# Attention's list with the last value group and the first output weights in it, measured durations, and both ScalarE tables loaded ahead of their stages

## The chip, the cores and the metric

One core of a Trainium2 chip runs the whole layer; seven stay unused. The metric is the device time of one execution in microseconds (us). TensorE is PE in the tables (its weight loads PEld), VectorE DVE, ScalarE ACT, GpSimd POOL, and SyncE SP, which issues nearly all DMAs. Every recorded operation goes through one helper, so nearly all rows carry line 183 (DMAs 177); they are told apart by their tiles.

## The reference

A decoder layer for 1024 tokens of width 1024. What matters here is the mixer:

```
h = x * (1 + scale1) + shift1
q, k, v, u, iq, ik, iw = split(h @ w_in)            # 8 heads of 64, 512 pooling channels, an indexer
score = sum over 8 index heads of iw * relu(rope(iq) @ rope(ik).T / 8), causal
keep the 256 highest scores of each token
p = softmax(rope(q) @ rope(k).T / 8 over the kept tokens);  attn = p @ v
x = layer_norm(alpha * x + gate1 * (concat(attn, pooled) @ w_o))
x = layer_norm(alpha * x + gate2 * ((silu(h2 @ w_gate) * (h2 @ w_up)) @ w_down))
```

## The kernel before, in words

Tokens are eight tiles of 128 (tile 7 is the last). Products are float32 split into a high and a low part, three matmuls for one; a split is an ACT copy (high) and a subtraction on DVE or POOL (low). The order of the instructions on an engine is that of the program where the engine is in the set `pinned`; where it is not, the framework may move an instruction ahead.

First come the modulation and the indexer's scores. For each tile from 2 to 7 the 256th highest score is then searched in generators (`bisect`, `mask_steps`, `drop_eights`), which yield the engine and cost of their next step. Tiles 7 and 6 are searched on DVE, 5 and 4 and then 3 on ACT by Sign activations, tile 2 on DVE by dropping eights (17 passes of a maximum and a replacement). The end of each is the mask: an equality, a count, a scan and 16-bit products, which write the bias for the softmax over the scores.

Beside the searches PE works through 24 `groups`: eight of pooling, eight of k, eight of v (loop of `PAIRS`); a function `fill` puts search steps into the holes that a running estimate of time (`Times`, `Queue.cost`) sees. A group is 24 matmuls of 512 columns. In the last group, number 23, `hold` stops the Sign steps and all chains but that of tile 7.

Attention is then a list. There are 32 units, a pair of heads (even and odd) by a tile of queries, grouped by g = 3, 2, 1, 0 (tiles 7 and 6, 5 and 4, and so on). A unit is a chain of tasks: s (scores, PE), x (bias and maximum, DVE, one for each head), e (exponent with its sum, ACT), r (reciprocal, DVE), n (norm, POOL), p (transposes, PE), c (copy out of PSUM, ACT or DVE), and for each two units o (values, PE) with hi (ACT) and lo (DVE). q tiles 5 to 0 come back from DRAM and are turned (load on SP, turn on PE, own and other on ACT, low on DVE). What is left of the three search chains are Chain objects in the same list. The list goes by one loop: each task's earliest time follows from the clocks of its engine and from its inputs' modelled ends; of those within SPAN us of the earliest, the one of lowest rank (its place in the units plus PRIO of its kind; for chains CHAIN_PRIO's first value plus a step for each of theirs) is written out. V_BIAS is added to a copy's time on DVE when the two engines are compared. Scores take two buffers of PSUM (ring B, two slots for over 512 columns), the others four (ring A). TensorE, DVE, ACT and POOL are pinned in the list.

The scaled probabilities lie in smr and the transposed ones in ptb, both in area H over hT, which group 23 still reads. Behind the list come the output weights: wo_load (an SP load, and a multiplication by gate1 on POOL) and wo_split, WO[0] and WO[1] in area V, the rest over k and v. Raw weights and q tiles share three buffers (RAW). After the list, weights are unpinned. The output projection starts with three tiles' products, k by k; then normalisation and the FFN, whose first Silu stands far behind.

Of the kernel before, what the change touches and what calls it, by code (L numbers as in the profile page):

```python
# [20 lines left out]
P = 128  # L21
# [22 lines left out]
V_BIAS = -0.075  # L44
SPAN = 0.106
PRIO = {'load': -387, 'turn': -49, 'own': -168, 'low': -13, 'other': -88, 's': 3, 'x': -36, 'e': 1, 'r': 152, 'n': -121, 'p': 12, 'c': 332, 'o': -134, 'hi': -115, 'lo': 145}
CHAIN_PRIO = {2: (500, 22.3), 3: (347, 6.4), 4: (-732, 10.2)}
# [148 lines left out]
def decoder_layer_kernel(  # L196
# [376 lines left out]
    def mask_steps(i, T1, ng, eq, lt):  # L573
        n, sc, w = P * (i + 1), score(i), (i + 1) / 8
        yield "V", 1.7 * w + 0.1
# [4 lines left out]
        yield "V", 1.6 * w  # L580
# [3 lines left out]
        yield "V", 1.8 * w  # L584
# [5 lines left out]
    def drop_eights(i, cols):  # L590
# [6 lines left out]
        for r in range((n - TOPK) // 8):  # L597
            yield "V", 1.0
            V.max(m8, neg)
            V.match_replace(neg, m8, neg, -3.4e38)  # L600
# [421 lines left out]
    last = len(groups)  # L1022
    pinned.clear()
# [12 lines left out]
    for s_ in (last, last + 1):  # L1036
        for f in late.pop(s_, []):
            f()
    assert not late, late
    def cat_slot(g):  # L1040
        return WS[g]
# [80 lines left out]
    def wo_load(k):  # L1122
        wo_raw[k] = raw_slot()
        SP.dma_start(wo_raw[k], wo_in[k])
        G.tensor_tensor(wo_raw[k], wo_raw[k], GR, ALU.mult)

# [57 lines left out]
    q_done, q_turns = {7: (), 6: ()}, []  # L1184
    masked = {0: 0.0, 1: 0.0}

    def q_rows(t, rank):
# [27 lines left out]
        t_ = task("turn", "T", 0.55, rank, turn, (l_,), "A", late=0.2)  # L1215
# [4 lines left out]
        t_.masks = {1: (3,), 0: (4, 5)}.get(t, ())  # L1220
        q_done[t] = (c1, lw)
        q_turns.append(t_)

    def unit(k):
# [31 lines left out]
        for e in (0, 1):  # L1256
            for j0 in range(0, i + 1, 4):
# [17 lines left out]
                c = task("c", "AV", (0.09 + 0.11 * m, 0.09 + 0.13 * m), 10 * k + 3, c_, [p] + list(o_tasks[-2:-1]), late=0.1)  # L1275
# [11 lines left out]
    for k in range(0, nu, 2):  # L1287
# [14 lines left out]
        o_t = task("o", "T", 0.1 + 0.865 * (g + 1), 10 * k + 14, o_, cs, "A", late=0.3)  # L1302
# [4 lines left out]
    class Chain:  # L1307
# [5 lines left out]
        def step(self):  # L1313
# [48 lines left out]
    while todo or chains:  # L1362
# [768 lines left out]
```

## Time and profile before

| what | value |
|---|---|
| median of 3 runs | 1252.07 us (1249.63 to 1252.88) |
| the profiled execution | 1250.99 us, of it 1249.2 us span of instructions |
| busy: PE, DVE, ACT, POOL | 1180.4, 1002.0, 656.0, 709.3 us |
| group 23 | about 328 to 334 us of the span |
| attention's list | about 334 to 472 us |
| output projection | from 468 us |
| ACT table loads | 4 of 1.28 us |

A profile's times are those of one execution. Busy time of PE is not its peak: matmuls overlap, their duration in a row is their latency. The granted clock is the share of PE's full clock: 1.0 is 2.4 GHz, 0.5 is 1.2 GHz, and a value between them is a mean of stretches at either.

### The profile page before, as it was taken

How to read it: one execution, taken by the hardware profiler on the slowest of the kernel's cores; microseconds unless marked ns; L12 is line 12 of the kernel's file. 1: busy time of each engine (PE TensorE's matmuls, PEld its weight loads, DVE VectorE, ACT ScalarE, POOL GpSimd, SP SyncE). 2: the span in 40 equal slices, each digit the busy share in tenths (PEclk: the TensorE clock that was granted, in tenths of full speed). 3: DMA queues.
4: the chain of work that ended last, by engine and by line, in shares of the span. 5: the costliest groups of instructions: out<-in, count | busy, mean ns of one | idle time of the engine just before them, and what ended most of it. 6: DMA issues, size and time to landing. Idle time of an engine off the chain costs nothing.

```text
span 1249.2 us, 16310 instructions
## 1 busy us (share of the span) xinstructions
PE 1180.4 (94%) x5622; PEld 919.8 (74%) x5622; DVE 1002.0 (80%) x1772; ACT 656.0 (53%) x1330; POOL 709.3 (57%) x505
## 2 busy tenths in 40 slices
PE   8999989999888899997899999999999999999996
PEld 6756556687665568876778787877878787878775
DVE  6799997988989975686977878787777768687698
ACT  4667878787789683455343434333333333442521
POOL 0093484676034362286784838475665748486848
PEclk9999999999989899997999999999999999999998
DMA  9610167421101035001312111112102020213212
GB/s 349 251 49 11 47 242 280 154 70 60 43 1 35 34 134 174 39 9 34 102 34 68 34 68 34 68 34 67 68 34 72 32 99 23 81 34 101 68 51 118
DMA packets 32459, 103.40 MB, mean 83 GB/s; under 512 B 3572, under 2 KB 3572, under 8 KB 28792
## 3 DMA queue, kind: packets, MB, share of 16 engines
q1 hardware_dynamic: 32376, 102.36, 23.1%
q8 instruction: 44, 0.72, 0.2%
q14 instruction: 39, 0.32, 0.1%
HBM read 92.90 MB, written 9.45 MB: 82 GB/s over the span
## 4 chain that ended last, share of the span: by engine, by line
PE 38%; DVE 7%; POOL 5%; issue 2%; ACT 1%; DVEq 0%; POOLq 0%; ACTq 0%
PE gu L183 23%; PE dn L183 15%; DVE act_W L183 2%; DVE utmp_X L183 2%; POOL wraw_R L183 1%; POOL wblk_T L183 1%; POOL wraw_W L183 1%; POOL wblk_V L183 1%; DVE gtmp_V L183 1%; DVE wblk_T L183 1%; DVE hr_H L183 0%; POOL hr_H L183 0%; DVE stat_C L183 0%; DVE wblk_V L183 0%; DVE res_X L183 0%
## 5 line engine op out<-in xcount | busy, mean ns | idle before, releaser
L183 PE MATMUL gu<-hr_H,wblk_T 128*128 128x512 f32 (+1 forms) x924 | 216.9, 387 | 2.6 <-ACT gtmp_V L183 2.3
L183 PE MATMUL gu<-hr_H,wblk_V 128*128 128x512 f32 (+1 forms) x924 | 215.1, 384 | 2.4 <-ACT gtmp_V L183 1.7
L183 PEld LDWEIGHTS gu<-hr_H,wblk_T 128*128 128x128 f32 x924 | 171.7, 190 | 38.7 <-ACT gtmp_V L183 2.9
L183 PEld LDWEIGHTS gu<-hr_H,wblk_V 128*128 128x128 f32 x924 | 170.0, 188 | 38.6 <-ACT gtmp_V L183 2.2
L183 DVE TENSOR_TENSOR res_X<-res_X,dn 128x512 f32<-128x512 f32 (+1 forms) x253 | 158.5, 675 | 15.4 <-PE dn L183 15.3
L183 POOL TENSOR_TENSOR wraw_R<-wraw_R 128x512 f32<-128x512 f32 x64 | 93.9, 1475 | 45.8 <-DVE wblk_T L183 23.1
L183 POOL TENSOR_TENSOR wraw_W<-wraw_W 128x512 f32<-128x512 f32 x60 | 85.8, 1437 | 55.8 <-DVE wblk_V L183 27.4
L183 PE MATMUL pj<-ws_W,hT_H 128*128 128x512 f32 x456 | 115.7, 400 | 1.0 <-DVE ws_W L183 1.0
L183 POOL TENSOR_SCALAR sm_H<-sm_H,stat_X 128x1024 f32<-128x1024 f32 (+7 forms) x64 | 49.1, 783 | 96.9 <-DVE stat_X L183 83.0
L183 PEld LDWEIGHTS pj<-ws_W,hT_H 128*128 128x128 f32 x456 | 83.0, 188 | 24.9 <-issue 6.5
L183 PE MATMUL dn<-wblk_T,act_W 128*128 128x512 f32 x324 | 79.4, 393 | 1.9 <-POOL wblk_T L183 1.2
L183 PE MATMUL dn<-wblk_V,act_W 128*128 128x512 f32 x324 | 78.8, 392 | 1.1 <-POOL wblk_V L183 1.1
L183 DVE TENSOR_SCALAR_CACHE_REDUCE junk_X<-keysD_T,colsD_X 128x1024 int16<-128x1024 int16 (+1 forms) x64 | 79.4, 1268 | 0.2
L183 ACT ACTIVATE wblk_V<-wraw_R 128x512 fp32r<-128x512 f32 x56 | 35.2, 629 | 80.7 <-POOL wraw_R L183 69.1
L183 PEld LDWEIGHTS dn<-wblk_T,act_W 128*128 128x128 f32 x324 | 60.1, 188 | 17.4 <-POOL wblk_T L183 3.9
L183 ACT ACTIVATE wblk_V<-wraw_W 128x512 fp32r<-128x512 f32 x53 | 33.1, 628 | 75.9 <-POOL wraw_W L183 62.4
L183 PEld LDWEIGHTS dn<-wblk_V,act_W 128*128 128x128 f32 x324 | 60.2, 188 | 16.2 <-POOL wblk_V L183 3.9
L183 ACT ACTIVATE wblk_T<-wraw_W 128x512 fp32r<-128x512 f32 x56 | 35.0, 628 | 65.9 <-POOL wraw_W L183 53.8
L183 ACT ACTIVATE wblk_T<-wraw_R 128x512 fp32r<-128x512 f32 x52 | 32.5, 627 | 61.3 <-POOL wraw_R L183 51.3
L183 PE MATMUL pT<-const_C,sm_H 128*128 128x128 f32 x288 | 45.2, 299 | 15.7 <-POOL sm_H L183 8.2
L183 DVE SCALAR_TENSOR_TENSOR score_X<-relu_K,const_C,score_X 128x384 f32<-128x384 f32 (+5 forms) x42 | 54.1, 1289 | 5.0 <-ACT relu_K L183 1.3
L183 ACT ACTIVATE utmp_X<-gu 128x512 f32<-128x512 f32 x33 | 19.7, 598 | 73.0 <-PE gu L183 73.0
(301 smaller groups left out, 2717.4 us busy)
## 6 DMA issues: line engine op xcount, KB each, us to landing
mset_K<-in_wmr_dram SPq DMA_DIRECT2D x16, 1024.0 KB, 5.3
wm_K<-in_wma_dram SPq DMA_DIRECT2D x16, 512.0 KB, 10.2
wraw_R<-in_wg_dram SPq DMA_DIRECT2D x6, 1024.0 KB, 4.7
wraw_R<-in_wd_dram SPq DMA_DIRECT2D x12, 512.0 KB, 3.6
wraw_W<-in_wup_dram SPq DMA_DIRECT2D x12, 512.0 KB, 3.5
wraw_R<-in_wup_dram SPq DMA_DIRECT2D x10, 512.0 KB, 3.6
wraw_W<-in_wg_dram SPq DMA_DIRECT2D x5, 1024.0 KB, 4.8
wraw_W<-in_wd_dram SPq DMA_DIRECT2D x10, 512.0 KB, 3.5
```

The costliest lines, as they stand in the source:

```text
L183: ins_ = f(*a, **k)
```

## The change

Group 23 leaves the loop and becomes the task vg of the list (with the copies va of group 22 and vb of group 23). Unit 0 has buffers of its own (sm_first). The x of later units, the first copies c, and turns of q tiles above 2 wait for vg. Loads and gates of output weights 0 to 2 and the splits of 0 and 1 become tasks; SP stays pinned in the list; a load is not written out before the one in front of it. Costs, ranks, V_BIAS and SPAN change. Ahead of a transposition p with a foreseen hole of more than 0.5 us on PE, KEEP times the rest of the hole is filled with transposes of the identity. One-column activations load ACT's tables: Exp at group 22, Silu at the end of the list.

```diff
-V_BIAS = -0.075
-SPAN = 0.106
-PRIO = {'load': -387, 'turn': -49, 'own': -168, 'low': -13, 'other': -88, 's': 3, 'x': -36, 'e': 1, 'r': 152, 'n': -121, 'p': 12, 'c': 332, 'o': -134, 'hi': -115, 'lo': 145}
-CHAIN_PRIO = {2: (500, 22.3), 3: (347, 6.4), 4: (-732, 10.2)}
+V_BIAS = 0.15
+KEEP = 0.55
+SPAN = 0.15
+PRIO = {'load': 650, 'turn': 53, 'own': -1350, 'low': -687, 'other': 600, 's': -261, 'x': -1371, 'e': 71, 'r': -915, 'n': 1966, 'p': -227, 'c': 659, 'o': -951, 'hi': -1034, 'lo': 641, 'gate': -895, 'group': 863, 'take': 1269, 'whi': -1001, 'wlo': -635}
+CHAIN_PRIO = {2: (1157, 15.6), 3: (1224, 52.0), 4: (1044, 55.3)}
...
-        yield "V", 1.7 * w + 0.1
+        yield "V", 1.7 * w + 0.1, False, 1.7 * w + 0.5
...
-        yield "V", 1.6 * w
+        yield "V", 1.6 * w, False, 3.4 * w
...
-        yield "V", 1.8 * w
+        yield "V", 1.8 * w, False, 2.9 * w
...
-            yield "V", 1.0
+            yield "V", 1.24
...
-    for n_, (kind, a, b) in enumerate(groups):
-        if n_ == len(groups) - 1:
-            hold.append(1)
+    for n_, (kind, a, b) in enumerate(groups[:-1]):
...
+        if n_ == 22:
+            at_(n_, lambda: A.activation(colsE[:, 16:17], ident[:, 0:1], AF.Exp))
...
-    last = len(groups)
-    pinned.clear()
+    last = len(groups) - 1
...
+    (take_22,) = late.pop(last)
+    sm_first = [buf("X", 5312, 1024, "sm"), buf("V", 7168, 1024, "sm")]
...
+    vg = task("group", "T", 3.4, 0, group_23, (), "A", late=0.2)
+    va = task("take", "A", 0.55, 0, take_22, (), late=0.1)
+    vb = task("take", "A", 0.55, 0, lambda: v_take(groups[-1][1], got["pp"]), (vg,), late=0.1)
...
-        t_ = task("turn", "T", 0.55, rank, turn, (l_,), "A", late=0.2)
+        t_ = task("turn", "T", 0.55, rank, turn, (l_, vg) if t > 2 else (l_,), "A", late=0.2)
...
-        s_t = task("s", "T", 0.2 + 0.0014 * n, 10 * k - EAGER, s_, q_done[i], "B" if n <= 512 else "BB", late=0.2)
+        s_t = task("s", "T", 0.1 + 0.0014 * n, 10 * k - EAGER, s_, q_done[i], "B" if n <= 512 else "BB", late=0.2)
-        xs = [task("x", "V", 0.08 + 0.00105 * n, 10 * k, lambda e=e: x_(e), [s_t] + before, late=0.12) for e in (0, 1)]
+        xs = [task("x", "V", 0.08 + 0.00105 * n, 10 * k, lambda e=e: x_(e), [s_t] + before + [vg] * (k > 0), late=0.12) for e in (0, 1)]
...
+                    for _ in range(spare):
+                        T.transpose(pt[:, 0:P], ident, ident)
...
-                c = task("c", "AV", (0.09 + 0.11 * m, 0.09 + 0.13 * m), 10 * k + 3, c_, [p] + list(o_tasks[-2:-1]), late=0.1)
+                c = task("c", "AV", (0.09 + 0.11 * m, 0.09 + 0.13 * m), 10 * k + 3, c_, [p] + (list(o_tasks[-2:-1]) or [vg]), late=0.1)
...
+        if k == 0:
+            turns[2].deps = list(turns[2].deps) + ps
...
-        o_t = task("o", "T", 0.1 + 0.865 * (g + 1), 10 * k + 14, o_, cs, "A", late=0.3)
+        o_t = task("o", "T", 0.865 * (g + 1) - 0.1, 10 * k + 14, o_, cs + [va, vb] * (g == 3), "A", late=0.3)
...
-            self.cost = (0.95 if self.q == "A" else 1.08) * self.st[1][1]
+            self.cost = self.st[1][3] if len(self.st[1]) > 3 else (0.9 if self.q == "A" else 1.02) * self.st[1][1]
...
+    for k in range(3):
+        d_ = task("load", "S", 0.1, 200, lambda k=k: wo_dma(k), (q_turns[3 + k],), late=5.0)
+        g_ = task("gate", "G", 2.35, 200 + k, lambda k=k: wo_gate(k), (d_,), late=0.15)
+        if k < 2:
+            h_ = task("whi", "A", 1.05, 205 + k, lambda k=k: wo_hi(k), [g_] + o_tasks[3:4], late=0.1)
+            task("wlo", "V", 1.15, 206 + k, lambda k=k: wo_lo(k), (h_,))
...
+        if t.kind == "p":
+            gap = at - max(clock[q], rings["A"].ready(1))
+            spare = max(0, int(KEEP * (gap - 0.5) / 0.11))
...
+    A.activation(colsE[:, 17:18], ident[:, 0:1], AF.Silu)
     pinned.clear()
-    wo_load(0)
-    wo_split(0)
-    wo_load(1)
-    wo_load(2)
     times.fill = None
-    wo_split(1)
     wo_split(2)
```

## Rows read from the trace of the kernel before

**Rows 1.** Windows of attention's list. Columns: the stretch, its length, then for PE, PEld, DVE, ACT and POOL the busy time and in brackets the instructions, then the granted clock, the DMA share and GB/s.
```profile
334.00:345.00 11.00, 7.39 (x36) 4.69 (x34) 8.30 (x19) 10.72 (x21) 2.22 (x2) 0.81 0.22 73
345.00:360.00 15.00, 11.72 (x59) 8.34 (x58) 13.28 (x27) 12.93 (x26) 4.20 (x4) 0.80 0.00 0
360.00:380.00 20.00, 19.20 (x152) 13.79 (x151) 18.93 (x45) 18.12 (x43) 8.48 (x8) 1.00 0.00 2
380.00:400.00 20.00, 17.83 (x139) 12.06 (x137) 17.61 (x43) 18.02 (x44) 7.78 (x7) 1.00 0.12 39
400.00:420.00 20.00, 17.27 (x111) 11.67 (x111) 18.55 (x45) 14.89 (x37) 10.69 (x8) 0.83 0.11 42
420.00:440.00 20.00, 15.28 (x89) 10.21 (x90) 19.28 (x53) 13.44 (x31) 9.46 (x10) 0.91 0.08 27
440.00:460.00 20.00, 20.00 (x164) 14.04 (x166) 14.71 (x48) 14.89 (x45) 13.04 (x19) 1.00 0.52 185
460.00:472.50 12.50, 12.29 (x92) 8.50 (x89) 7.08 (x38) 9.26 (x38) 4.99 (x12) 1.00 0.24 86
```

**Rows 2.** PE's timeline at the start of the list: start, length, engine, operation, and in brackets the idle time before it with its releaser. The first row holds groups 22 (end) and 23.
```profile
322.69 11.18 PE L183 MATMUL pj<-ws_W,hT_H 128*128 128x512 f32 x48
...
342.60 1.11 PE L183 MATMUL pT<-const_C,sm_H 128*128 128x128 f32 x4 [2.84 <-POOL sm_H L183]
...
348.76 0.63 PE L183 MATMUL pT<-const_C,sm_H 128*128 128x128 f32 x4 [1.15 <-ACT qab_W L183]
...
352.08 0.66 PE L183 MATMUL pT<-const_C,sm_H 128*128 128x128 f32 x4 [0.95 <-DVE pT_H L183]
353.87 4.70 PE L183 MATMUL pT<-const_C,sm_H 128*128 128x128 f32 x26 [1.13 <-DVE pT_H L183]
```

**Rows 3.** ACT's timeline around it: a Sign step (junkB), the last copy of v, the table load and the first exponent.
```profile
323.10 0.72 ACT L183 ACTIVATE junkB_X<-keysA_X,colsA_X 128x512 bf16<-128x512 uint16 x1 [1.54 <-DVE colsA_X L183]
...
333.91 0.60 ACT L183 ACTIVATE vf_V<-pj 128x512 f32<-128x512 f32 x1 [4.42 <-PE pj L183]
...
337.38 1.28 ACT L183 ACT_TABLE_LOAD   x1
338.67 1.15 ACT L183 ACTIVATE sm_H<-sm_H,stat_X 128x1024 f32<-128x1024 f32 x1
```

**Rows 4.** DVE's timeline, the two largest holes of 334 to 345 us.
```profile
341.08 0.17 DVE L183 RECIPROCAL stat_X<-stat_X 128x2 f32<-128x2 f32 x1 [0.85 <-ACT sm_H L183]
...
344.57 2.81 DVE L183 TENSOR_TENSOR qab_W<-qT,qab_W 64x512 fp32r<-64x512 f32 x4 [1.32 <-ACT qab_W L183]
```

**Rows 5.** Groups of instructions over the whole run, the table loads: busy time, mean ns, idle time before and its releasers.
```profile
L183 ACT ACT_TABLE_LOAD x4 | 5.1, 1283 | 2.6 <-DVE gtmp_V L183 1.8 <-PEq L2119 0.7
```

**Rows 6.** The tile pT, its copies on both engines: shortest, median and longest in ns, first and last start.
```profile
L183 ACT ACTIVATE pT_H<-pT x51: 262/493/616, 354.9 to 471.1; 128x512 f32<-128x512 f32 x24, 128x384 f32<-128x384 f32 x10, 128x128 f32<-128x128 f32 x9, 128x256 f32<-128x256 f32 x8
L183 DVE COPY pT_H<-pT x45: 270/670/692, 351.3 to 470.9; 128x512 f32<-128x512 f32 x24, 128x256 f32<-128x256 f32 x8, 128x128 f32<-128x128 f32 x7, 128x384 f32<-128x384 f32 x6
```

**Rows 7.** The tile raw from 280 to 480 us, the gate multiplications of output weights, columns as in rows 6.
```profile
L183 POOL TENSOR_TENSOR raw_R<-raw_R,gr_G x5: 2367/2372/2391, 389.3 to 451.2; 128x1024 f32<-128x1024 f32 x5
```

**Rows 8.** Timelines of POOL, then DVE, then PE about 417 us: a gate, mask steps of tile 3, PE's next work.
```profile
417.14 2.37 POOL L183 TENSOR_TENSOR raw_R<-raw_R,gr_G 128x1024 f32<-128x1024 f32 x1 [2.92 <-PE pT L183]
...
417.35 2.44 DVE L183 TENSOR_TENSOR keysA_X<-keysA_X,score_X 128x512 bf16<-128x512 bf16 x1
419.83 0.43 DVE L183 TENSOR_TENSOR junkB_X<-junkB_X,keysA_X 128x512 bf16<-128x512 bf16 x1
...
422.40 2.21 PE L183 MATMUL pT<-const_C,sm_H 128*128 128x128 f32 x10 [3.34 <-POOL sm_H L183]
```

**Rows 9.** Timelines of POOL, then DVE: the next gate, and the mask steps of tile 2 from its scan on.
```profile
429.14 2.39 POOL L183 TENSOR_TENSOR raw_R<-raw_R,gr_G 128x1024 f32<-128x1024 f32 x1 [5.91 <-issue]
...
426.00 1.01 DVE L183 TENSOR_TENSOR_SCAN score_X<-neg_X,colsE_X 128x384 bf16<-128x384 bf16 x1
427.05 0.26 DVE L183 TENSOR_SCALAR score_X<-score_X 128x384 bf16<-128x384 bf16 x1
...
430.21 1.54 DVE L183 TENSOR_TENSOR neg_X<-neg_X,score_X 128x384 bf16<-128x384 bf16 x1
431.78 0.94 DVE L183 TENSOR_TENSOR neg_X<-neg_X 128x384 bf16<-128x384 bf16 x1
432.76 0.95 DVE L183 TENSOR_SCALAR score_X<-neg_X 128x384 f32<-128x384 bf16 x1
```

**Rows 10.** ACT's timeline in the FFN, the last table load and the first Silu.
```profile
589.86 1.28 ACT L183 ACT_TABLE_LOAD   x1 [1.81 <-DVE gtmp_V L183]
591.15 0.72 ACT L183 ACTIVATE gtmp_V<-gtmp_V 128x256 f32<-128x256 f32 x2
```

**Rows 11.** PE's timeline behind it.
```profile
593.82 1.22 PE L183 MATMUL gu<-hr_H,wblk_V 128*128 128x256 f32 x8 [0.36 <-POOL hr_H L183]
596.42 3.92 PE L183 MATMUL gu<-hr_H,wblk_T 128*128 128x256 f32 x18 [1.38 <-ACT gtmp_V L183]
```

**Rows 12.** Timelines of ACT and PE at the end of the list: the splits of weights 2 to 4, and PE's first matmuls with weights 2 and later (tile hr).
```profile
472.64 2.94 ACT L183 ACTIVATE hr_H<-raw_R 128x1024 fp32r<-128x1024 f32 x3
...
478.96 7.42 PE L183 MATMUL wo<-hr_H,ws_W 128*128 128x512 f32 x32
```

**Rows 13.** PE's timeline after the mask of tile 2.
```profile
435.11 1.16 PE L183 MATMUL s<-kr_K,qab_H 128*128 128x512 f32 x4 [0.90 <-DVE stat_X L183]
```

More of the change, by code (lines that the diff above doesn't have):

```diff
@@ L1035, in decoder_layer_kernel @@
     smr = buf("H", 8192, 6144, "sm")
-    for s_ in (last, last + 1):
-        for f in late.pop(s_, []):
-            f()
+    (take_22,) = late.pop(last)
     assert not late, late
+    sm_first = [buf("X", 5312, 1024, "sm"), buf("V", 7168, 1024, "sm")]
     def cat_slot(g):
@@ L1120, in decoder_layer_kernel, with wo_dma, wo_gate, wo_load @@
     wo_raw = {}
-    def wo_load(k):
+    def wo_dma(k):
         wo_raw[k] = raw_slot()
         SP.dma_start(wo_raw[k], wo_in[k])
+    def wo_gate(k):
         G.tensor_tensor(wo_raw[k], wo_raw[k], GR, ALU.mult)
+    def wo_load(k):
+        wo_dma(k)
+        wo_gate(k)
     def wo_split(k):
@@ L1144, in pool_split @@
             V.tensor_tensor(lo, src, f_(hi), ALU.subtract)
+    loads = []
     class Task:
@@ L1149, in __init__ @@
             self.q, self.cost, self.rank, self.emit, self.deps, self.slots, self.late = q, cost, rank + PRIO[kind], emit, deps, slots, late
-            self.end, self.kind, self.masks = None, kind, ()
+            self.end, self.kind, self.masks, self.behind = None, kind, (), loads[-1:] if kind == "load" else []
+            if kind == "load":
+                loads.append(self)
     class Ring:
@@ L1176, in decoder_layer_kernel @@
         n = P * (u[2] + 1)
-        if n > 512:
+        if u == units[0]:
+            sm_of[u] = sm_first, {6}
+        elif n > 512:
             sm_of[u] = [smr[:, (o + e) % 6 * 1024 :][:, 0:n] for e in (0, 1)], {o % 6, (o + 1) % 6}
@@ L1183, in decoder_layer_kernel, with group_23 @@
     sm_users, live = {}, {}
-    q_done, q_turns = {7: (), 6: ()}, []
+    q_done, q_turns, turns = {7: (), 6: ()}, [], {}
     masked = {0: 0.0, 1: 0.0}
+    got = {}
+    def group_23():
+        got["pp"] = psA("pj")
+        t_f(groups[-1][1])(got["pp"], range(KT))
+    vg = task("group", "T", 3.4, 0, group_23, (), "A", late=0.2)
+    va = task("take", "A", 0.55, 0, take_22, (), late=0.1)
+    vb = task("take", "A", 0.55, 0, lambda: v_take(groups[-1][1], got["pp"]), (vg,), late=0.1)
+    vg.readers = (vb,)
+    rings["A"].free[-1][0] = 1.0
     def q_rows(t, rank):
@@ L1220, in q_rows @@
         t_.masks = {1: (3,), 0: (4, 5)}.get(t, ())
+        turns[t] = t_
         q_done[t] = (c1, lw)
@@ L1259, in unit, with p_ @@
                 hold_ = {}
-                def p_(e=e, j0=j0, m=m, hold_=hold_):
+                def p_(spare=0, e=e, j0=j0, m=m, hold_=hold_):
                     hold_["pt"] = pt = psA("pT")
+                    for _ in range(spare):
+                        T.transpose(pt[:, 0:P], ident, ident)
                     for j in range(m):
@@ L1317, in step, with wo_hi, wo_lo @@
             self.q = self.st[1][0]
-            self.cost = (0.95 if self.q == "A" else 1.08) * self.st[1][1]
+            self.cost = self.st[1][3] if len(self.st[1]) > 3 else (0.9 if self.q == "A" else 1.02) * self.st[1][1]
+    def wo_hi(k):
+        A.activation(WO[k][:, 0:1024], wo_raw[k], AF.Copy)
+    def wo_lo(k):
+        V.tensor_tensor(WO[k][:, 1024:2048], wo_raw[k], f_(WO[k][:, 0:1024]), ALU.subtract)
+    for k in range(3):
[4 more added lines that the diff above has]
+            task("wlo", "V", 1.15, 206 + k, lambda k=k: wo_lo(k), (h_,))
     t0 = T.t
@@ L1335, in earliest @@
             at = max(at, d.end)
+        if any(b.end is None for b in t.behind):
+            return FAR
         for i in t.masks:
@@ L1380, in decoder_layer_kernel @@
             kind[0] = t.kind
+        spare = 0
+        if t.kind == "p":
+            gap = at - max(clock[q], rings["A"].ready(1))
+            spare = max(0, int(KEEP * (gap - 0.5) / 0.11))
         if t.slots:
             t.got = rings[t.slots[0]].take(len(t.slots))
-        t.emit(q) if len(t.q) > 1 else t.emit()
+        if spare:
+            t.emit(spare)
+        else:
+            t.emit(q) if len(t.q) > 1 else t.emit()
         clock[q] = at + cost
```

## The prediction

> **What bounds the kernel now.** I read first the windows of the attention stage, then PE's timeline there, then ACT's and DVE's around each PE hole, last the place of the FFN where the second table is loaded. The windows say that the stage has two limits [rows 1]. From 334 to 440 us DVE is busy 8.30 + 13.28 + 18.93 + 17.61 + 18.55 + 19.28 = 95.95 of 106 us, ACT 88.12, PE 88.69; PE's share moreover holds half-clock work (mean granted clock 0.80 to 0.83 in three of the stretches). From 440 us on PE is full (20.00 of 20.00, 12.29 of 12.50) and DVE has air. So up to 440 us the list is worth what it saves on DVE; after that PE's work (32.5 us) can only begin earlier. PE can follow such a shift: it sits idle 106 - 88.69 = 17.3 us before 440.
>
> The stage's start is the worst part. Group 23 (half of the 11.18 us row of 48 matmuls, 5.6 us) ends at 333.9, only then does unit 0 begin, and its chain scores, x, exponent, norm, transpose must run through before the pipe is full: PE waits 2.84, 1.15, 0.95 and 1.13 us, partly at half clock [rows 2]. On ACT the Sign steps are held back during group 23 (4.42 us idle), and the exponent's table is loaded between the first x and the first exponent, 1.28 us [rows 3]. DVE's idle time from 334 to 360 us is 2.70 + 1.72 = 4.42 us [rows 1]; its pieces end with ACT's results [rows 4].
>
> **The change, part by part.**
>
> *Group 23 in the list.* Unit 0's scores need nothing of the group, and by the list's rule (earliest first, then rank) they go out before it; unit 0 now has buffers outside hT's area, the x of all others wait for the group. So x, exponent and norm of unit 0 run beside 5.6 us of PE work instead of beside a waiting PE. The bound is DVE, whose work does not shrink: what can go is its idle time, 4.42 us. Ends: 0 (the hole only moves) and 5.6 (the whole group hidden). I take 4.4, nearer to the upper end, since PE's holes alone (6.07 us) exceed the group.
>
> *Exponent's table.* Its load goes to group 22, where ACT had a hole of 1.54 us ahead of a Sign step [rows 3]; if that hole is gone it costs a Sign chain 1.28 us, and PE nothing. The gain lies in the 4.4 already. Relu, Sign and Copy alternate with exponents and Silu in the whole kernel at four loads [rows 5], so nothing is reloaded. The lifted hold on the Sign chain, 4.4 us of ACT, is credited with nothing: ACT is not the bound.
>
> *Copies.* The bias of 0.15 us against DVE (before 0.075 for it) sends copies of transposed probabilities to ACT. 45 run on DVE, median 0.67 us, the largest 0.69; on ACT the largest take 0.62 [rows 6]. The busy times differ by 95.95 - 88.12 = 7.8 us [rows 1], one moved large copy closes 0.69 + 0.62 = 1.31, so six level them and take 4.1 us off DVE. Ends 0 and 4.1; I take four median copies, 2.7 us, since some will meet an ACT that is not free.
>
> *Output weights 0 to 2 in the list.* Three loads on SP, three gate multiplications on POOL of 2.37 us [rows 7], two splits on ACT and DVE. All ran within the attention before, put there by the framework, so no work is added. Behind a gate on POOL stand the norms, and behind them PE's transposes; behind a load on SP, which keeps its order in the list now, only the next loads. The danger is what a gate meets. The one at 417.14 ran beside a DVE mask step of two 16-bit inputs: 2.44 us, where the next of the same shape took 0.43; PE then stood still for 3.34 us until the norm came [rows 8]. Beside the gate at 429.14 and the norm behind it the last three steps of tile 2 took 1.54, 0.94 and 0.95 [rows 9]. Against the 0.43 of the larger tile that is 1.11 + 0.51 + 0.52 = 2.1; with the 2.0 at 417 it is 4.1 us of DVE. The Trainium skill (GPSIMD Engine Reference, Key points) says that GpSimd shares its SBUF interfaces with VectorE and contends with its two-input and two-port instructions: the trace agrees with 2.44 against 0.43, and by that rule gates fixed in the list speak against the change wherever they fall on mask steps. Where they fall now the trace cannot show. Ends: 4.1 gained (no meeting) and 4.1 lost (two more); I take 0, since as many gates and mask steps remain.
>
> *Durations, ranks.* A drop step costed at 1.08 us becomes 1.26 (1.24 x 1.02), mask steps up to double. I credit that with nothing of its own: it brings the list nearer to the chip, but DVE, busy 95.95 of 106 us [rows 1], leaves little to order. Ends: the 5.6 us of DVE idle time from 360 to 440 us gained, or as much again lost.
>
> *Spare transposes.* PE transposes the identity ahead of a foreseen hole, to hold the clock. The 0.81 and 0.80 granted from 334 to 360 us [rows 1] mean about 10.2 us at 1.2 instead of 2.4 GHz, 5.1 us of PE work, but PE is not the bound there. Ends: 2.2 us gained (DVE's idle time from 400 to 440 us, the other stretches of a lowered clock) and 1.1 us lost (six spare ones at the 0.18 us of the 26 transposes at 353.87 [rows 2], ahead of holes that don't come). I take 0: PE's 17.3 idle us hide them; without that cover they cost the 1.1.
>
> *Silu's table.* The load leaves the FFN. At 589.86 it stands between DVE's product and the first Silu [rows 10]; PE waits 0.36 and 1.38 us for work that queued behind it [rows 11]. Ends 0 and 1.28; I take 1.2, as the waits exceed it. The new place is the end of the list: 472.6, ahead of the split of weights 2, the first of three on ACT of about 1 us each; PE needs it at 478.96 [rows 12]. With a DVE half of about the same length it is done by 476.4 instead of 474.9. So 1.5 us of 4 us of cover are used; if that cover were gone it would cost 1.5.
>
> The Trainium skill (ScalarE: Activation LUTs, What ACT_TABLE_LOAD costs) puts a drain of about 1.38 us on top of each load. By it the two loads would be worth 5.3 us in place of 2.6, and the time would be an estimated 1.4 us lower, for Silu's alone. The rows at 337 and 589 show 1.28 us and the next ACTIVATE at once [rows 3, 10]; the measurement decides.
>
> **Sum.** 4.4 + 2.7 + 1.2 = 8.3 us. The profiled execution took 1250.99 (span 1249.2 and 1.8 around it), 1.1 below the median of the three runs, 1252.07, inside their spread. 1250.99 - 8.3 = **1242.7 us**.
>
> **Rivals.**
>
> *The masks come late (slower).* Chains rank behind everything in the list now (from 1044 upward, copies from 662 to 972), so DVE takes a chain step only when nothing else is ready. Scores of units 16 and 17 do not wait for masks, their x do: if masks 3 and 2 are not there when units 0 to 15 are through, both score buffers fill with waiting scores and PE stops. For it: PE already waited 0.90 us for such a buffer at 435.11, just after mask 2 [rows 13]. Against it: the list plans those steps, with longer costs than before. It decides once the last steps stand alone on DVE. Price: scan to bias of tile 2 uncovered, 1.01 + 0.26 + 1.54 + 0.94 + 0.95 = 4.7 [rows 9], and of tile 3 by its length 4/3 of that, 6.3, an estimate; moved copies then bring nothing: 1250.99 - 4.4 - 1.2 + 11.0 = 1256.4.
>
> *The gain at the start is given back.* Unit 0 starts early, but the x of unit 1 waits for group 23 as before, so the hole appears behind it; copies moved to ACT make its exponents late. For it: only unit 0 has buffers of its own, and ACT is busy 88.12 of 106 us [rows 1]. Only Silu's 1.2 remains: 1249.8.
>
> *The list as a whole gets better.* No gate on a mask step, six copies moved: 5.6 + 4.1 + 4.1 + 1.28 = 15.1, so 1235.9. For it: PE has 17.3 idle us to give [rows 1]. Against it: all ends at once.
>
> *It does not do what it says.* A table load that stays where it was, or a second one by a later exponent: 1.28 or 2.6 us less gain, 1244.0 or 1245.3, within the forecast's own case.
>
> **Numbers.** Forecast 0.60 (with the last rival in it), whole list better 0.10, given back 0.18, masks late 0.12. A measurement of this kernel can tell about 0.3% from no change, 3.8 us. The first two are faster, 0.70; the third is the same, 0.18; the last slower, 0.12. Range: from 1236 (nearly all gain ends) to 1254, which takes in given back and the lesser half of masks late.
>
> **What would show it.** Right: scores of unit 0 ahead of the matmuls of group 23, the first PE hole after them under 1 us, clock 1.0 through the first 25 us; no table load at the first exponent nor at the first Silu; fewer than 45 copies on DVE; stage end 7 us earlier, and FFN stretches of the same length but for 1.2 us. Wrong: as much DVE idle time up to the masks as before, PE idle around masks 3 and 2 by several us, or gates that lengthen mask steps again.

## The result and the profile after

The kernel after takes 1238.99 us (median of 5 runs, 1238.61 to 1241.15) against 1252.07 before: ratio 0.990, interval 0.9886 to 0.9915, a gain of 12.5 us (10.6 to 14.3). Measured again later, unchanged (run e9), it took 1242.14 (6 runs, 1238.63 to 1244.00) against 1251.37: ratio 0.9922 (0.9904 to 0.994), a gain of 9.8 us (7.5 to 12.0). The forecast was 1242.7, faster; both medians lie in its range. The profiled execution took 1238.72 (span 1236.7), 12.27 below the profiled one before.

Where the 12.3 us of the two profiled executions came from can be read at three places. PE's first matmul with weights 2 (tile hr) starts at 466.15 instead of 478.96 [rows 12]: 12.8 us are gained by the end of the list. The stage of the output projection (wo) gives 1.6 of it back. The FFN gains 1.1 around its first Silu. The windows of the list, in the stretches and columns of [rows 1]:

```profile
334.00:345.00 11.00, 7.37 (x40) 4.70 (x38) 10.80 (x22) 9.69 (x19) 2.23 (x2) 1.00 0.14 49
345.00:360.00 15.00, 14.27 (x94) 10.17 (x95) 12.94 (x30) 14.43 (x27) 7.37 (x8) 0.89 0.06 17
360.00:380.00 20.00, 19.91 (x158) 14.25 (x157) 19.09 (x46) 18.93 (x46) 7.99 (x8) 1.00 0.01 2
380.00:400.00 20.00, 19.50 (x157) 14.32 (x155) 18.26 (x50) 19.09 (x51) 7.30 (x10) 1.00 0.00 1
400.00:420.00 20.00, 18.09 (x133) 12.11 (x131) 18.47 (x48) 19.16 (x44) 8.02 (x8) 1.00 0.08 27
420.00:440.00 20.00, 18.21 (x117) 12.17 (x117) 16.77 (x62) 16.92 (x47) 13.98 (x16) 0.91 0.34 120
440.00:460.00 20.00, 19.38 (x154) 13.48 (x153) 11.32 (x47) 15.91 (x57) 12.83 (x21) 1.00 0.46 171
```

The reader sees three things. PE is busy 97.33 of the 106 us from 334 to 440, 8.6 more than before. ACT is busy 98.22 and now stands level with DVE, 96.33. And DVE has air already from 420 to 440 us, 16.77 of 20, where before it was full.

The whole list next, once for each kernel, from 328 us to its end (before: 472.50, after: 459.50):

```profile
328.00:472.50 144.50, 126.99 (x858) 88.25 (x858) 123.52 (x321) 113.82 (x282) 60.86 (x69) 0.93 0.15 54
```
```profile
328.00:459.50 131.50, 122.22 (x867) 85.26 (x866) 113.19 (x307) 119.25 (x297) 59.72 (x69) 0.97 0.16 55
```

Of 13.0 us less, 10.3 are less DVE work and 2.7 less DVE idle time (20.98 to 18.31). ACT took over 5.4. Two things make up nearly all of DVE's 10.3. The first is the copies of transposed probabilities, in the columns of [rows 6]:

```profile
L184 ACT ACTIVATE pT_H<-pT x65: 272/574/632, 348.7 to 458.1; 128x512 f32<-128x512 f32 x34, 128x256 f32<-128x256 f32 x12, 128x128 f32<-128x128 f32 x10, 128x384 f32<-128x384 f32 x9
L184 DVE COPY pT_H<-pT x31: 279/548/691, 345.8 to 454.9; 128x512 f32<-128x512 f32 x14, 128x384 f32<-128x384 f32 x7, 128x128 f32<-128x128 f32 x6, 128x256 f32<-128x256 f32 x4
```

Fourteen moved, not the four of the forecast; DVE spends 15.7 us on the rest where it spent 23.5. The second is the mask steps, POOL's timeline first and then DVE's:

```profile
411.47 2.39 POOL L184 TENSOR_TENSOR raw_R<-raw_R,gr_G 128x1024 f32<-128x1024 f32 x1 [7.30 <-DMA raw_R<-in_wo_dram]
423.84 2.38 POOL L184 TENSOR_TENSOR raw_R<-raw_R,gr_G 128x1024 f32<-128x1024 f32 x1 [6.50 <-DVE stat_X L184]
...
408.36 0.35 DVE L184 TENSOR_TENSOR neg_X<-neg_X,score_X 128x384 bf16<-128x384 bf16 x1
408.74 0.36 DVE L184 TENSOR_TENSOR neg_X<-neg_X 128x384 bf16<-128x384 bf16 x1
415.65 1.04 DVE L184 TENSOR_SCALAR keysA_X<-score_X,colsA_X 128x512 bf16<-128x512 f32 x1
420.44 0.41 DVE L184 TENSOR_TENSOR keysA_X<-keysA_X,score_X 128x512 bf16<-128x512 bf16 x1
```

The steps that took 2.44, 1.54, 0.94 and 0.95 us [rows 8, 9] take 0.41, 0.35, 0.36 and 0.36. The gates fall just after tile 2's mask and just after tile 3's, and none falls on one of these steps. One step beside norms on POOL became longer, 1.04 (0.49 before). By their rows the copies are 7.8 us shorter and the four steps 4.4. That is more than 10.3, because busy time counts the overlap of neighbouring instructions once.

PE's and ACT's timelines at the start, to read beside [rows 2, 3]:

```profile
328.35 1.73 PE L184 MATMUL s<-kr_K,qab_V 128*128 128x512 f32 x8
330.01 5.74 PE L184 MATMUL pj<-ws_W,hT_H 128*128 128x512 f32 x24
...
338.73 1.09 PE L184 MATMUL pT<-const_C,sm_X 128*128 128x128 f32 x8 [0.39 <-POOL sm_X L184]
...
345.28 2.29 PE L184 MATMUL pT<-const_C,sm_V 128*128 128x128 f32 x8 [3.25 <-issue]
```
```profile
328.98 1.28 ACT L184 ACT_TABLE_LOAD   x1
...
334.81 1.16 ACT L184 ACTIVATE sm_X<-sm_X,stat_X 128x1024 f32<-128x1024 f32 x1 [0.99 <-DVE stat_X L184]
...
343.99 2.41 ACT L184 ACTIVATE qab_W<-qT 64x512 fp32r<-64x512 f32 x4
```

Unit 0's scores stand ahead of group 23 and its first transposes are there 3.9 us earlier, with a wait of 0.39 instead of 2.84. The table is loaded beside unit 0's scores. But the hole has not gone: PE stands still for 3.25 us between the transposes of unit 0's two heads (tiles sm_X and sm_V), and the clock falls there (0.76 from 344 to 346 us, 0.50 from 346 to 348).

The profile names no releaser for this wait ("issue"), but the times point to one. The second head's norm had ended on POOL at 339.79. Its transposes need two of ring A's four PSUM buffers; two hold the first head's transposes, two those of q tiles. The last readers of the q tiles' buffers are ACT's copies `other`, the row at 343.99, which stand behind unit 1's exponents: the second of the four ends at 345.18, the last at 346.40. PE goes on at 345.28 and, for the other buffer, at 346.45.

At the end of the list, ACT's and then PE's timeline:

```profile
459.73 1.28 ACT L184 ACT_TABLE_LOAD   x1
...
466.15 8.32 PE L184 MATMUL wo<-hr_H,ws_W 128*128 128x512 f32 x36
...
487.02 0.73 PE L184 MATMUL wo<-hr_H 128*128 128x512 f32 x2 [0.31 <-ACT hr_H L184]
488.45 3.92 PE L184 MATMUL wo<-hr_H 128*128 128x512 f32 x16 [0.69 <-DVE hr_H L184]
492.21 1.52 PE L184 MATMUL wo<-wo_V,ws_W 128*128 128x512 f32 x6
```

From weights 2 to the next row block PE now takes 26.06 us; before it was 24.48 (478.96 to 503.44). It waits for the splits of the last weights, on both engines. In the FFN, ACT and PE again (compare [rows 10, 11]):

```profile
578.64 0.73 ACT L184 ACTIVATE gtmp_V<-gtmp_V 128x256 f32<-128x256 f32 x2 [1.81 <-DVE gtmp_V L184]
...
587.49 1.70 PE L184 MATMUL gu<-hr_H,wblk_W 128*128 128x256 f32 x12 [1.05 <-ACT gtmp_V L184]
...
598.11 5.60 PE L184 MATMUL gu<-hr_H,wblk_V 128*128 128x512 f32 x24
```

No table load stands in front of Silu. PE's row just before it came 11.23 us earlier than in the kernel before (580.14, 591.37 before), the row at 587.49 (600.14) 12.65, and the row at 598.11 (610.46) 12.35. So 1.4 us are gained at the Silu, and 1.1 of them are left ten us later.

### The profile page after: what moved, and what is told of

It reads as the page before. It is cut to its first block, busy times and chain, and to the rows that moved or that the text cites. A ratio compares the mean times of both kernels' runs of the same rounds, so it can differ in the third digit from the quotient of the medians.

```text
span 1236.7 us, 16336 instructions
## 1 busy us (share of the span) xinstructions
PE 1176.7 (95%) x5631; PEld 917.1 (74%) x5631; DVE 990.6 (80%) x1758; ACT 661.4 (53%) x1346; POOL 708.1 (57%) x505
## 4 chain that ended last, share of the span: by engine, by line
PE 38%; DVE 7%; POOL 5%; issue 2%; ACT 1%; DVEq 0%; POOLq 0%; ACTq 0%
PE gu L184 23%; PE dn L184 15%; DVE act_W L184 2%; DVE utmp_X L184 2%; POOL wraw_R L184 1%; POOL wblk_T L184 1%; POOL wraw_W L184 1%; POOL wblk_V L184 1%; DVE gtmp_V L184 1%; DVE wblk_T L184 1%; DVE hr_H L184 0%; POOL hr_H L184 0%; DVE stat_C L184 0%; DVE wblk_V L184 0%; DVE res_X L184 0%
## 5 line engine op out<-in xcount | busy, mean ns | idle before, releaser
L184 POOL TENSOR_SCALAR sm_H<-sm_H,stat_X 128x896 f32<-128x896 f32 (+7 forms) x62 | 45.8, 755 | 44.1 <-DVE stat_X L184 31.5
L184 ACT ACTIVATE junkA_T<-keys_T,colsA_X 128x768 bf16<-128x768 uint16 (+3 forms) x62 | 54.4, 877 | 3.8 <-DVE colsA_X L184 2.9
```

The lines of the kernel that those rows point to most:

```text
L184: ins_ = f(*a, **k)
```

## The experiments

All stand beside runs of the kernel before on their own chip; one gain in us is one ratio times 1251. The theory was: the list gains because DVE's work shrinks (copies, mask steps without gates) and because unit 0 runs beside group 23; Silu's table adds 1 us. The rivals were that another part carries it, or that the gain is one of order alone.

| run | edit | median us | ratio, interval | against before, us |
|---|---|---|---|---|
| e1 | before + Silu's table early | 1250.46 | 0.9997 (0.9986 to 1.0007) | -0.4 |
| e2 | before, no gates of weights 0 to 4 | 1246.79 | 0.9969 (0.9957 to 0.998) | -3.9 |
| e3 | before, 14 copies to ACT | 1252.05 | 1.0011 (1.0002 to 1.002) | +1.4 |
| e4 | after, Silu's table later | 1240.28 | 0.9919 (0.9906 to 0.9933) | -10.1 |
| e5 | after, 14 copies back to DVE | 1244.74 | 0.9949 (0.9937 to 0.9961) | -6.4 |
| e6 | after, group 23 first | 1242.90 | 0.9939 (0.992 to 0.9958) | -7.6 |
| e7 | after, two more multiplications on masks | 1244.75 | 0.9949 (0.9936 to 0.9963) | -6.4 |
| e8 | after, exponent's table not ahead | 1242.14 | 0.9927 (0.9908 to 0.9946) | -9.1 |
| e9 | after, unchanged | 1242.14 | 0.9922 (0.9904 to 0.994) | -9.8 |
| e10 | after, no spare transposes | 1241.48 | 0.9917 (0.9902 to 0.9932) | -10.4 |
| e11 | before, new durations and ranks | 1253.59 | 1.0014 (1.0 to 1.0028) | +1.8 |
| e12 | before, new durations | 1248.40 | 0.9976 (0.9967 to 0.9985) | -3.0 |

**The copies.** e3 issues fourteen of DVE's copies, every second one of four and of two blocks, on ACT, in the order of the old list; e5 gives as many of the same sizes back in the new one.

```diff
 # e3, before (shortened)           # e5, after: the same with "A" -> "V", every third
-        t.emit(q) if len(t.q) > 1 else t.emit()
+        if q == "V" and m in (4, 2):          # m: blocks in the copy
+            seen[m] += 1
+            if seen[m] % 2 == 0 and seen[m] <= {4: 20, 2: 8}[m]:
+                q = "A"
```

> The old kernel, its list written out in the same order, but 14 copies of transposed probabilities (10 of 512 columns, 4 of 256) that the list gave to DVE are issued on ACT at the same place: 31 on DVE, 65 on ACT as in the changed kernel. Theory (DVE is the bound up to 440 us, ACT has 18 us of air): DVE's busy time falls by 8 us, the time by 3 to 6 us. Rival (ACT is as near to the bound, the exponents come later by what the copies take): within 1.5 us of before, or slower; then only a list planned with the moved copies gains from them.

> The changed kernel, its list in the same order, but 14 copies that it gave to ACT (10 of 512 columns, 4 of 256) issued on DVE at the same place, so that 45 run there as before. Theory (less DVE work is the largest part of the gain): DVE's busy time in the list rises by about 8 us and the time by 4 to 8 us over 1239. Rival (the order makes the gain, not the engine): under 2 us.

e3 is 1.4 us slower, e5 loses 3.4 us against e9 and 6.1 against the first measurement of the kernel after; its interval lies apart from the first's and overlaps e9's at the edge. In e5's trace, from 334 to 440 us, DVE is busy 97.94 us (96.33 in the kernel after), and PE only 93.89 (97.33) at the same mean clock of 0.97: the price is paid where DVE is nearly full. The same window of e3 says why fourteen copies bring nothing alone:

```profile
334.00:440.00 106.00, 87.56 (x589) 58.65 (x588) 90.78 (x219) 92.51 (x209) 43.08 (x38) 0.95 0.09 28
```

DVE is busy 5.2 us less than the 95.95 of [rows 1], ACT 4.4 more than 88.12, and PE did no more work: DVE's freed time is idle time. 2.3 us of it are waits for ACT's Sign steps, which now stand in a fuller queue (the groups of DVE's lines put 3.7 us of idle ahead of the drop steps' first operation, 1.4 before). That e3 is slower, and not only no faster, its trace doesn't show: the list begins 1.8 us later than before (group 22 at 324.46, 322.69 before) and ends 0.4 later (479.37, 478.96). So fourteen moved copies were worth something only in a list that was ordered with them.

**The gates.** e2 leaves out the gate multiplication of output weights 0 to 4 (their product lacks that factor). e7 lets POOL read one column of masks 2 and 3 between two of their steps and then multiply a spare buffer of 1024 columns.

```diff
 # e2, before
-        G.tensor_tensor(wo_raw[k], wo_raw[k], GR, ALU.mult)
+        if k > 4:
+            G.tensor_tensor(wo_raw[k], wo_raw[k], GR, ALU.mult)
 # e7, after, in mask_steps behind `left`
+        if i in (2, 3):
+            G.tensor_scalar(colsE[:, 18:19], left[:, 0:1], 1.0, None, ALU.mult)
+            G.tensor_tensor(meet, meet, GR, ALU.mult)
```

> The old kernel without GpSimd's multiplications of output weights 0 to 4 by the gate (left out, the output projection is then computed without that factor for these), so no gate can meet a mask step of tiles 3 and 2. Theory (mask steps beside a gate were lengthened by some 4 us, and DVE was the bound): the steps that took 2.44 and 1.54 us take about 0.42 and 0.35, the time falls by 2 to 4 us. Rival (the list only waits elsewhere): under 1 us, though the steps are short.

> The changed kernel with two more multiplications of 1024 columns on GpSimd (the size of a gate), each tied to the mask of tile 2 or 3 so that it runs beside its 16-bit products. Theory (a meeting lengthens DVE's two-input 16-bit steps several times, as at 417 us in the old kernel): a step beside each takes 1.5 to 2.4 us instead of 0.35 to 0.43, the time rises by 2 to 4 us over 1239. Rival (DVE has air there now, 18 us in the list): steps lengthened, time within 1 us.

Without gates the kernel before gains 3.9 us (2.5 to 5.4), for shorter mask steps and a shorter queue on POOL together, and the first step behind the scan of tile 3 takes 0.43 instead of 2.44, as POOL's and DVE's timelines of e2 show:

```profile
427.30 1.88 POOL L183 TENSOR_SCALAR sm_H<-sm_H,stat_X 128x768 f32<-128x768 f32 x2 [7.23 <-DVE stat_X L183]
...
416.16 0.43 DVE L183 TENSOR_TENSOR keysA_X<-keysA_X,score_X 128x512 bf16<-128x512 bf16 x1
...
427.43 0.98 DVE L183 TENSOR_TENSOR neg_X<-neg_X 128x384 bf16<-128x384 bf16 x1
```

The last row is long without any gate, 0.98 against 0.36 in the kernel after: a norm on POOL lies beside it. So a gate is not the only work that lengthens such a step.

With two more on the masks (e7) the list after loses 3.4 us against e9, 6.1 against the first measurement. Here the price is paid at another place than I said. POOL, then PE, then DVE in e7:

```profile
419.22 1.05 POOL L184 TENSOR_SCALAR colsE_X<-score_X 128x1 f32<-128x1 bf16 x1 [3.24 <-DVE score_X L184]
420.23 2.33 POOL L184 TENSOR_TENSOR sm_V<-sm_V,gr_G 128x1024 f32<-128x1024 f32 x1
422.54 1.57 POOL L184 TENSOR_SCALAR sm_H<-sm_H,stat_X 128x640 f32<-128x640 f32 x2
424.08 2.35 POOL L184 TENSOR_TENSOR raw_R<-raw_R,gr_G 128x1024 f32<-128x1024 f32 x1
...
423.39 2.40 PE L184 MATMUL pT<-const_C,sm_H 128*128 128x128 f32 x10 [6.16 <-POOL sm_H L184]
...
424.97 1.75 DVE L184 TENSOR_TENSOR keysA_X<-keysA_X,score_X 128x512 bf16<-128x512 bf16 x1
```

The step of tile 3 is 1.34 us longer than in the kernel after, tile 2's 0.72. (Tile 3's met the gate at 424.08; the added multiplication had ended before it.) But the norm of the next unit stands in POOL's queue behind the read and the multiplication, so PE waits 6.16 us, and DVE, whose next copy needs PE, 4.56. Of that, POOL itself stood 3.24 us, since the edit lets the read wait for the mask; the multiplication takes 2.33. Before tile 2's mask the two traces agree (its scan begins at 405.23, 405.19 in the kernel after), and the list ends 4.8 us later (470.97, 466.15). So the run mixes prices; it shows that what stands in front of a norm in POOL's queue costs more than the longer step.

**The start.** e6 issues group 23's matmuls ahead of unit 0's scores and leaves the rest of the list; e8 puts a Copy in the place of the early exponent, so the table is loaded at unit 0's exponent.

```diff
 # e6
-    vg = task("group", "T", 3.4, 0, group_23, (), "A", late=0.2)
+    vg = task("group", "T", 3.4, 0, lambda: None, (), "A", late=0.2)
+    group_23()                                # ahead of the loop over the list
 # e8
-            at_(n_, lambda: A.activation(colsE[:, 16:17], ident[:, 0:1], AF.Exp))
+            at_(n_, lambda: A.activation(colsE[:, 16:17], ident[:, 0:1], AF.Copy))
```

> The changed kernel, its list in the same order, but the matmuls of group 23 are written out ahead of unit 0's scores instead of behind them. Theory (the overlap of unit 0's softmax with the group is worth the idle time of DVE at the start, 2.7 to 4.4 us): x of unit 0 starts about as much later as the scores (5.6 us), 2.5 to 4.5 us over 1239. Rival (DVE has masks to do there and takes them first, the start is not what counts): under 1 us.

> The changed kernel, but the one-column activation at group 22 is a Copy instead of an Exp, so the exponent's table is loaded at the first exponent as before; nothing else differs. Theory (unit 0's softmax now runs beside 5.6 us of matmuls, so a later exponent is half covered): 0.3 to 1.3 us over 1239. Rival (fully covered, or ACT's bound is elsewhere): 0 within 0.3.

Neither interval lies apart from e9's. By the ratios e6 loses 2.2 us against e9 and 4.9 against the first measurement, with single runs from 1240.57 to 1247.34; e8 loses 0.7 and 3.4, with runs from 1238.79 to 1245.60. e8's trace speaks for no price at all: the load stands at 332.97, where ACT has nothing else to do, and the exponent behind it waits another 1.11 us for DVE. In e6's profile, PE's timeline has the group in one block again, and the hole comes four us later:

```profile
324.68 11.18 PE L184 MATMUL pj<-ws_W,hT_H 128*128 128x512 f32 x48
...
349.20 0.63 PE L184 MATMUL pT<-const_C,sm_V 128*128 128x128 f32 x4 [2.94 <-issue]
```

DVE's first copy is issued at 349.7 in e6 and at 345.8 in the kernel after, 3.9 us later. But 1.9 of that were there before the list (tile 7's scan begins at 306.20, 304.32 in the kernel after), so 2.0 us hang on the order of the group. By the times the price is 2 to 5 us and not clear of e9's spread.

**Silu's table.** e1 loads it at the end of the old list; e4 loads it behind the split of weights 4.

```diff
 # e1, before                         # e4, after: this line behind wo_split(4) instead
     pinned.clear()
+    A.activation(colsE[:, 17:18], ident[:, 0:1], AF.Silu)
     wo_load(0)
```

> The old kernel with one thing added: a one-column Silu on ScalarE at the end of attention's list, so that the table is loaded there and not in the FFN. Theory (the load stood in front of work that PE waits for, and its new place is hidden): 1.2 us less than before, no table load at the first Silu, PE's waits after it shrink from 0.36 + 1.38 us to under 0.9. Rival (hidden in the FFN anyway, or paid again at the list's end through later splits of the output weights): 0 to 0.5 us.

> The changed kernel, but the one-column Silu that loads the table waits for the split of output weights 4, so it stands behind the three splits and not ahead of them. Theory (PE's waits of 0.31 and 0.69 us for the last output weights at 487 and 488 us come in part from the 1.5 us that the load puts ahead of the chain of splits, raw buffers, loads and gates): 0.5 to 1.5 us less than the changed kernel's 1239.0, so about 1238. Rival (the chain is late by a gate that meets a DVE split): no difference, 1239 within 0.4.

In time e1 can't be told from no change, nor from -1.2. In its trace the load stands at 471.54, and PE's timeline has these rows:

```profile
498.93 3.92 PE L183 MATMUL wo<-hr_H 128*128 128x512 f32 x16 [0.19 <-DVE hr_H L183]
...
597.87 1.70 PE L183 MATMUL gu<-hr_H,wblk_W 128*128 128x256 f32 x12 [1.04 <-ACT gtmp_V L183]
...
602.35 7.38 PE L183 MATMUL gu<-hr_H,wblk_W 128*128 128x256 f32 x36 [2.06 <-ACT gtmp_V L183]
```

From the stage's first row (570.40; before 571.32) to the row at 597.87 (600.14) the FFN is 1.35 us shorter. But nothing of it is left ten us later: the row after the last one shown comes at 609.56 (610.46), 0.90 earlier, as the stage's first row does (0.92). The half clock lies on those 36 matmuls (0.50 from 603 to 605 us), where the kernel before ran the same work at full clock in 6.15 us (604.31 to 610.46). And in the wo stage PE waits 0.19 us for a split behind the table's load.

In e4, with the load later, PE has no hole in the wo stage at all: 470.60 to 495.08, 24.48 us as before. e8 and e10, whose lists end as late as e4's (470.24 and 470.35), have the load ahead of the splits and take 25.23 and 24.82 us there, so the load's share of the 1.6 us is 0.3 to 0.8. e5, e6 and e7 take 25.33 to 26.69 with lists that end no earlier; what makes up the rest is not shown.

e4's median, 1240.28, is no better than the kernel after's for all that: in its profiled execution the list itself ended 4.4 us later than in the kernel after, though its instructions up to there are the same. 1.8 us of that were there before 410 us (tile 2's scan begins at 406.99, 405.19 in the kernel after). Where the rest arose the clock says. PE, PEld, DVE, ACT, POOL, clock from 420 us on, the kernel after first, then e4:

```profile
420.00:425.00 5.00, 4.33 (x26) 2.85 (x26) 4.31 (x14) 2.79 (x9) 1.16 (x1) 0.66 0.28 105
425.00:430.00 5.00, 4.55 (x24) 2.44 (x22) 3.22 (x14) 4.29 (x13) 4.68 (x7) 1.00 0.01 2
430.00:435.00 5.00, 5.00 (x41) 3.54 (x40) 4.85 (x18) 4.92 (x13) 3.48 (x7) 1.00 0.50 177
```
```profile
420.00:425.00 5.00, 4.15 (x35) 3.00 (x36) 4.86 (x12) 2.96 (x9) 0.00 (x0) 1.00 0.31 105
425.00:430.00 5.00, 3.13 (x17) 1.89 (x17) 3.56 (x16) 5.00 (x16) 4.48 (x5) 0.99 0.01 2
430.00:435.00 5.00, 5.00 (x18) 3.14 (x18) 3.10 (x12) 2.23 (x6) 2.22 (x4) 0.50 0.00 0
435.00:440.00 5.00, 5.00 (x32) 3.26 (x30) 2.74 (x8) 4.18 (x11) 2.89 (x6) 0.83 0.62 212
```

In the one the half clock (1.2 GHz) falls on a stretch in which PE has holes anyway, and is over by 425. In the other it comes after two thin stretches (PE busy 4.15 of 5 and 3.13 of 5), and lies on 5 us in which PE is full: 18 matmuls in place of 41. The same stretch at 0.50 stands in the profiles of e8 and e10.

**Unchanged, and without spare transposes.** e9 is the kernel after again; e10 sets `KEEP = 0.0`, which takes out its nine transposes of the identity.

> The kernel after, unchanged, on the chip of this batch, to stand beside the runs that edited it. Theory: the edits of the second batch took the time that they show, so this comes out at 1239 to 1240, below all of them, and the clock between 420 and 440 us averages 0.9 or more. Rival: where the half clock falls in the list (0.5 from 430 to 435 us with Silu later and with Exp not ahead, 0.66 from 420 to 425 us here) differs by chip or run whatever the edit; then this comes out at 1241 to 1242.5 too, with a stretch at 0.5, and the 1 to 3 us of those two edits are not theirs.

> The kernel after without its nine spare transposes (the list is planned without them). Theory: they lie in one stretch of 1.20 us at 413.98, ahead of a hole of 1.22 us in which TensorE waits for ScalarE's copies, so without them TensorE waits longer and nothing ends sooner: 0 (from -1.2 to +0.5). Rival: they keep the clock up; without them the clock is at half for 7 us more and the time is 2 to 4 us longer.

The rival of e9 was right on the time, though not on the stretch at 0.5 in its profile: the kernel's own spread, 1238.6 to 1244.0, is as large as what e4, e6, e8 and e10 were to tell. Its profiled execution was the fastest of its six (1238.63) and has the clock of the first profile, 0.91 from 420 to 440, so that the slower executions of the unchanged kernel are those with the half clock later is probable and not shown. The nine transposes are worth nothing that can be measured.

**Durations and ranks on the old list.** e12 gives the planner of the kernel before the new durations alone, e11 the new bias, span and ranks as well; group 23, weights and tables stay where they were.

```diff
 # e12 (excerpt)
-        yield "V", 1.8 * w
+        yield "V", 1.8 * w, False, 2.9 * w
-            yield "V", 1.0
+            yield "V", 1.24
 # e11: e12 and the V_BIAS, SPAN, PRIO, CHAIN_PRIO of the kernel after
```

> The kernel before with only the new durations in its planner, ranks and bias as they were. Theory: with the ranks of the old list nothing is gained by durations alone, -1 to +2. Rival: the durations are what lets the planner keep the masks and the copies apart, and they bring most of what new ranks bring: -4 or better.

> The kernel before with the new durations, ranks and bias in its list, but the last value group, the first output weights and the tables where they were. Theory: what is planned with the new durations and ranks is worth the copies (6 us by the run that put them back) and part of the gates; the start (4 to 5 us) and Silu (1 us) are missing, so -4 to -7 against before. Rival: the ranks are made for a list with the group and the weights in it and do nothing or harm without them: -1 to +4.

Both came out against the theory. The durations alone gain 3.0 us (1.9 to 4.1), though only two copies move (43 stay on DVE). Gates move too: the first two stand at 343.36 and 347.25 (389.30 and 401.79 before), none lies on tile 3's mask (its first step, at 417.72, takes 0.42), and the one near tile 2's ends as its first step begins. POOL's timeline and DVE's:

```profile
425.39 2.38 POOL L183 TENSOR_TENSOR raw_R<-raw_R,gr_G 128x1024 f32<-128x1024 f32 x1 [5.64 <-issue]
...
427.53 0.46 DVE L183 TENSOR_TENSOR neg_X<-neg_X,score_X 128x384 bf16<-128x384 bf16 x1
```

With the ranks as well it is slower than before by 1.8 (0 to 3.5), although 13 copies moved. POOL, PE and DVE in e11:

```profile
419.59 4.67 POOL L183 TENSOR_TENSOR raw_R<-raw_R,gr_G 128x1024 f32<-128x1024 f32 x2 [8.64 <-DMA raw_R<-in_wo_dram]
...
426.17 3.63 PE L183 MATMUL pT<-const_C,sm_H 128*128 128x128 f32 x17 [5.73 <-POOL sm_H L183]
...
434.70 3.90 PE L183 MATMUL o<-pT_H,vf_V 128*64 128x256 f32 x22 [3.20 <-DVE pT_H L183]
...
429.07 2.47 DVE L183 TENSOR_SCALAR keysA_X<-score_X,colsA_X 128x512 bf16<-128x512 f32 x1
```

Two gates stand in a row ahead of the norms, and PE waits 5.73 us for those. Then tile 3's mask, 20 us later than before (409.06 there), keeps DVE from a copy, and PE waits 3.20 us more. The second is near to the forecast's slower rival (a late mask stops PE), here in a list without the group and the weights; the first is of the kind that e7 showed.

## Why the prediction was right

The direction, the time and the place were right: the list gained, by less DVE work and less DVE idle time up to 440 us [rows 1], and PE followed. The single terms were less good, and their errors cancelled in part, so that the hit is in part luck.

- **Group 23, 4.4.** The scores of unit 0 do stand ahead of the group. DVE's idle time from 334 to 360 us fell from 4.42 to 0.20 + 2.06 = 2.26, by 2.2 and not by all. PE kept a hole of 3.25 us, where I had said under 1 us and a full clock for 25 us. This is not the mechanism of the rival "given back": PE waits there not for the x of unit 1 but, by the times, for PSUM buffers that ACT's copies of the q tiles hold, which I had not counted. e6 puts the order of the group at 2.0 us in its trace and at 2 to 5 us in time, not clear of the spread.
- **Copies, 2.7.** Mis-sized, and beyond its upper end: DVE's copies are 7.8 us shorter, as fourteen moved where I thought that six would level the engines. The list went past level, ACT 98.22 against DVE 96.33. e5 gives them a price of 3.4 to 6.1 us; on the old order, in e3, they brought nothing (1.4 us slower).
- **Output weights, 0.** The choice failed: the steps of [rows 8, 9] take 1.48 us where they took 5.87, 4.4 us of DVE and a little over the upper end that I had named. Of these 3.2 are the two steps beside gates and 1.2 the two beside a norm, which e2 without gates leaves long (0.98 and 0.95). The trace agrees with the rule of the Trainium skill (GPSIMD Engine Reference, Key points) that GpSimd contends with VectorE's two-input instructions: with a multiplication of 1024 columns beside it the first step of tile 3 took 2.44 and 1.75 us, without one 0.41 to 0.43. The rule spoke against the change where gates fall on mask steps; in the new list they fall between the masks. I had also not counted POOL's queue: PE's hole of 3.34 us behind a gate and a norm [rows 8] is gone, and e7 and e11 show holes of 6.16 and 5.73 us of the same kind (e7's in part by its edit).
- **Durations and ranks, 0.** e12 gives the durations 3.0 us by themselves; its six steps behind the scans of masks 2 and 3 are 2.2 us shorter (4.58 to before's 6.73). So this is probably in part the cause of the term above, and no further one; no run takes the durations out of the new list. The ranks, with bias and span, belong to this list and cost some 5 us on the old one (e11 against e12).
- **Silu, 1.2.** Measured in the FFN: 12.35 less 11.23 us, 1.1; in e1, where the half clock falls just behind, 0. The cover I named at its new place did not hold in full: the list ended earlier, the weights did not by as much, and PE waited 0.31 and 0.69 us for splits; 1.6 us of the wo stage are lost. 0.3 to 0.8 of that is the table's load (e8 and e10 against e4), so the term is worth less than 1 us, and e1 can't tell it from nothing.
- **Exponent's table and spare transposes, 0.** e8 and e10 show no difference in time, as far as 3 us of spread let it be seen, and in e8's trace the load is covered. Right.
- **Sum.** DVE's busy time in the list fell by 10.3 us and its idle time by 2.7, 13.0 against the 7.1 forecast for the list. That is near "the whole list better", to which I gave 0.10. The first median lies 3.7 us below the forecast and the second, 1242.14, on it; the difference between the two is the spread of one kernel, so the second is no better proof of the terms.

## What to carry to other kernels

In a list in which one engine is full, count the work that leaves that engine, and plan again: fourteen copies moved in place brought nothing, in a list ordered for them they are worth several us. Measured durations in the planner paid 3.0 us by themselves, most likely because POOL's multiplications then lay off DVE's mask steps, and the ranks found for one set of tasks did not carry over to another. A gain read at one row is not yet a gain: follow it to the end, as in e1. Before a comparison of 1 to 3 us is believed, run the unchanged kernel again beside it, and look at which stretch the half clock has fallen on.

## What the runs showed of the hardware

One order of instructions takes two courses. With no other instruction ahead of its end, the list of e4 ended 4.4 us later than that of the kernel after: 1.8 us had built up before 410 us, and then the half clock lay on 430 to 437 us where PE was full, and not on 420 to 425 where it had holes. The mean clock of the run hardly shows it, 0.983 against 0.986.

A mask step that met an operation on POOL was not slowed in proportion: it ended 0.2 to 0.3 us behind the end of that operation, whenever it had begun. The step at 417.35 ended at 419.79 and the gate beside it at 419.51 [rows 8], the one at 430.21 at 431.75 and its gate at 431.53 [rows 9], e7's at 424.97 at 426.72 and its gate at 426.43. DVE's copies out of PSUM were not lengthened: the largest stayed at 0.69 us in every run.

The time between a table load's start and the next ACTIVATE was 1.28 to 1.30 us also at the new places (328.98 and 330.27; 459.73 and 461.03). The Trainium skill (ScalarE: Activation LUTs, What ACT_TABLE_LOAD costs) adds a drain of about 1.38 us; no row of these runs shows it.
